# Three rearrangements of TensorE's order: branch B's values two blocks behind their transpositions, pair weights loaded one pair sooner, branch A's transpositions two tiles behind

## The chip, the cores and the metric

The kernel runs on one core of a Trainium2 chip. Its engines work side by side, each through its own list of instructions, and wait for each other by semaphores: TensorE (PE; PEld is its loading of weights) multiplies, VectorE (DVE), ScalarE (ACT) and GpSimd (POOL) do the elementwise work, and SyncE (SP) issues the transfers. SBUF is the working memory, and PSUM holds what PE writes, in banks of 512 fp32 columns. The metric is the time of one execution on the device in microseconds, as the median of several; a profile is taken of one further execution.

## What is computed

One block of an encoder: 1024 tokens of width 1024 with 16 meta tokens ahead of them, all in fp32. Two attentions stand side by side on the normed input, and what they give is mixed by gates; a feed-forward part follows.

```python
def mixer_block(h, w_in, lq1, lk1, lq2, lk2, subln_g, sink, w_ba, w_bb, w_o, lambda_init):
    proj = h @ w_in                      # qa, ka, va, qb, kb, vb, ga, gb side by side
    ...
    y_a = differential_attention(...)    # 4 heads: softmax(q1 k1) - lam * softmax(q2 k2), times v, over all keys
    y_b = windowed_gqa(...)              # 8 heads in 2 groups, each block of 128 queries sees 3 blocks of keys
    merged = jax.nn.sigmoid(ga) * (y_a @ w_ba) + jax.nn.sigmoid(gb) * (y_b @ w_bb)
    return merged @ w_o

def reference(x, meta_tokens, ...):
    ...
        h = h + mixer_block(rms_norm(h, norm_mix[layer]), ...)
        h = h + swiglu(rms_norm(h, norm_ffn[layer]), w_ff_gate[layer], w_ff_up[layer], w_ff_down[layer])
    return rms_norm(h, norm_final)[:, N_META:]
```

## The kernel before

Every fp32 operand of a matmul is split into a rounded part (hi) and a rest (lo), and a product is made of three matmuls: hi hi, hi lo, lo hi. A split costs ACT a copy (the hi) and DVE or POOL a subtraction (the lo).

The mixer runs in stages, along PE's order. First come the normed input's transposes and the projections of branch B. Then **branch B** (65 to 246 us of the profile): for each of 2 groups and 8 blocks of 128 queries, `attend_b` gives two generators. `scoring` makes four scores (L329), whose exponentials ACT takes (L337) and POOL scales (L343). `values()` transposes the result key block by key block (L363, two to three blocks and one of meta tokens) into one of two PSUM banks (tile `bpt`), copies it to SBUF as hi (ACT, L365) and lo (DVE, L367) in one of four tiles `btr`, and multiplies it by v (`products`, L357); the sum of a block lies in the bank `bpy`. While block n is scored, block n-1 is transposed and multiplied: the list `finish` holds its generator. A string of letters sets PE's order within a block: `SLOTS_B`, where s takes a step of the scores, t one of the values and g one step of fill. Fill (`more`, from `fill_b`) is work that is needed later: projections of v and k of branch A (L214) in steps of three matmuls, whose results ACT and DVE take out.

What is left of the fill follows branch B. While it runs, DVE makes `token_sums` (L608 to L621), sums of quarters of the transposed input, split into the tiles `tops`. Then come the **pair products** (`product_t`, L690; 268 to 395 us and, before them, the end of the fill): pairs of 128 columns of q of branch A and of the gates, seven products each, made by Strassen-Winograd's scheme from sums of quarters. A pair's weights are two transfers (`load_t`, L651), which DVE combines (L660 to L664) and ACT and POOL split (`wop_t`). DVE also adds up the products (L699), and so frees their banks.

**Branch A** (395 to 660 us) takes 4 heads of 8 tiles of 128 queries. A step n of the loop makes tile n's six scores (two maps of three, L785, each into one bank of a ring of five, `SC`), which DVE adds the distances to (L788), ACT takes the exponential of (L793) and, of the second map, DVE combines with the first (L799). The same step transposes an earlier tile (`transpose_a`, L811: three banks of the same ring, taken out by ACT at L814 and DVE at L815), and for every second tile `values_a` multiplies by v (L824) and `normed_a` norms (L837 to L846). The order is set by the strings `SLOTS` for the first 13 steps and `SLOTS_LAST` after them, where s is a score, t a transposition, n a step of the values or the norm, g a fill step. The first map of a tile is scored into fresh tiles, the second into one of two that alternate (`s0s`). Each head's q and k are loaded by `load_a` (L761 to L764) into single tiles that the scores of the head before must have released.

The order is written out by hand for PE alone (`manual_schedule`); that of the other engines' instructions comes from a scheduler, which may place them otherwise when PE's order changes.

Of the kernel before, what the change touches and what calls it, by code (L numbers as in the profile page):

```python
# [9 lines left out]
F32 = mybir.dt.float32  # L10
# [10 lines left out]
P = 128  # L21
# [18 lines left out]
PC_BUFS = 8  # L40
PAD_T = 192
COMBINE_POOL = (0, 1, 2, 3)
SLOTS = "sgsgsngsgsstntnt"
SLOTS_LAST = "sgssngsgsstntnt"
N_MORE = 13
SLOTS_B = "sgsgsgsggttgttgttgtt"
S_BUFS = (2, 2)
AT_BUFS = 2
G_BUFS = 3
# [8 lines left out]
QK_BUFS = 3  # L58
W_BUFS = 2
X_BUFS = 2  # L60
T_LAG = 1
V_AT = 2
B_LAST = 10
E_STEPS = 1
OP_BUFS = 8
# [13 lines left out]
def encoder_block(ctx: ExitStack, tc: tile.TileContext, x, meta, norm_mix, w_in, lq1, lk1, lq2, lk2,  # L79
# [78 lines left out]
    wpool, close_wpool = pool("wpool", "right")  # L158
# [155 lines left out]
    def attend_b(g, t, finish):  # L314
# [35 lines left out]
        def values():  # L350
# [9 lines left out]
            for k, kp, o in blocks:  # L360
                pt = bank(psum1, "bt", f"bpt_{nm}_{k}", 2).rearrange("p (r t) -> p r t", r=4)
                for r in range(4):
                    nc.tensor.transpose(pt[:kp, r, :], st[:, r, o:o + P] if k < 8 else md[:, r], ident)  # L363
                tr = bpool.tile([P, 2, 4, P], F32R, tag="btr", name=f"btr_{nm}_{k}", bufs=4)
                nc.scalar.activation(tr[:kp, 0], pt[:kp], AF.Copy)  # L365
                lo = tr[:, 1] if k < 8 else tr[:NM, 0]
                nc.vector.tensor_tensor(lo, pt[:lo.shape[0]], f32(tr[:lo.shape[0], 0]), ALU.subtract)  # L367
                trs.append((k, kp, tr))
                yield
                if len(trs) > 1:  # L370
                    products(*trs.pop(0))
                    yield
            products(*trs.pop(0))
            y1 = bpool.tile([64, 512], F32, tag="by1", name=f"by1_{nm}", bufs=2)
            nc.scalar.copy(y1, py[64:128])
# [203 lines left out]
    order_pe = tc.manual_schedule(engines={mybir.EngineType.PE})  # L579
    order_pe.__enter__()  # L580
    more = fill_b()
    for _ in finish.pop(0):
        next(more)
    for n in range(2, BG * NT):
# [60 lines left out]

    def load_t(u):
        for kh in range(2):
            p = tpool if u % 2 else wpool
            w = raw_t[u, kh] = p.tile([P, 4, 2 * P], F32, tag="w", name=f"wt_{u}_{kh}", bufs=2)
            src = w_in[kh * 512:kh * 512 + 512, units[u][0]:units[u][0] + 2 * P]  # L650
            nc.sync.dma_start(w, src.rearrange("(c p) n -> p c n", p=P))  # L651

# [46 lines left out]
            nc.vector.tensor_tensor(other, ps, other, ALU.add)  # L699
            result_t(u, *{2: (0, 0), 7: (1, 1), 3: (0, 1)}[p], other)  # L700

    load_t(0)
    load_t(1)
    for n, (u, p) in enumerate(steps_t):
        while len(ops_t) < min(len(steps_t), n + 2 * W_BUFS):
            ahead = steps_t[len(ops_t)]
            weights_t(*ahead)
            if ahead[1] == 4 and ahead[0] + 2 < len(units):
                load_t(ahead[0] + 2)
        product_t(u, p)  # L710
    order_pe.__exit__(None, None, None)
    order += order_fill
# [809 lines left out]
```

## Time and profile before

| | us |
|---|---|
| median of 3 runs (lowest to highest) | 1510.72 (1507.9 to 1513.98) |
| profiled execution | 1509.8 |
| its span, first to last instruction | 1508.0 |
| PE busy in the span | 1449.7 |
| PE busy, 65 to 246 us (branch B) | 166.7 of 181 |
| PE busy, 268 to 395 us (pair products) | 114.1 of 127 |
| PE busy, 395 to 660 us (branch A) | 255.6 of 265 |

Times within the profile are microseconds from the span's start. A row of a timeline has the start, the length, the engine, the line of the kernel, the operation, what it writes and reads, and in square brackets how long its engine was idle before it and whose result ended that. A row of the list of waits has who waits for whom, the sum in us, how often, and the longest.

### The profile page before, as it was taken

The page shows a single profiled execution, that of the slowest core. Times are in us where ns is not written, and L with a number is a line of the kernel's source. Part 1 is how long each engine was busy: PE and PEld are TensorE (multiplying, and loading weights), DVE is VectorE, ACT ScalarE, POOL GpSimd, SP SyncE. Part 2 cuts the span into 40 slices and gives each one's busy share as a digit, 9 for nine tenths or more (in the row PEclk, how much of TensorE's full clock was granted, in tenths as well). Part 3 has the DMA queues.
Part 4 walks back from the last instruction along what each step waited for, and adds up shares of the span by engine and source line. Part 5 has one row for each costly group of instructions (what it writes and reads, how often), then busy time and mean ns, then how long its engine had stood idle before and what let it go on. Part 6 is the DMA issues. An engine that isn't in the chain of part 4 may idle for free.

```text
span 1508.0 us, 21007 instructions
## 1 busy us (share of the span) xinstructions
PE 1449.7 (96%) x7315; PEld 1229.4 (82%) x7315; DVE 895.3 (59%) x1635; ACT 685.2 (45%) x1296; POOL 565.0 (37%) x555
## 2 busy tenths in 40 slices
PE   8999999799999999999999999999999999999998
PEld 7877779578898898987878878888888888888886
DVE  6456666831497787824443495655555554778666
ACT  6365654433365555625532463333333333444444
POOL 4243432544232322322663316454544453000344
PEclk9999999999999999999999999999999999999999
DMA  7424313352714424128662254333333232864443
GB/s 231 91 59 113 84 58 112 97 147 89 220 58 149 134 79 127 51 86 263 196 216 76 79 154 159 108 105 105 105 105 102 101 105 105 291 240 126 133 126 140
DMA packets 154203, 193.13 MB, mean 128 GB/s; under 512 B 16288, under 2 KB 98656, under 8 KB 154096
## 3 DMA queue, kind: packets, MB, share of 16 engines
q1 hardware_dynamic: 154096, 191.78, 40.0%
q8 instruction: 58, 0.95, 0.3%
q14 instruction: 49, 0.40, 0.1%
HBM read 131.24 MB, written 53.94 MB: 123 GB/s over the span
## 4 chain that ended last, share of the span: by engine, by line
PE 75%; DVE 7%; issue 5%; DMA 5%; POOL 4%; ACT 3%; SPq 1%; POOLq 0%; DVEq 0%; ACTq 0%
PE pg L1303 27%; PE pd L1397 8%; PE po L1069 6%; PE pp_g L214 5%; PE pt L690 5%; PE ppa L728 4%; PE aps L785 3%; PE apy L824 3%; POOL oa L121 3%; PE apt L811 2%; PE pp_qb L214 2%; PE pp_ka L214 2%; PE pp_va L214 2%; PE bpy L357 1%; DVE btr L367 1%
## 5 line engine op out<-in xcount | busy, mean ns | idle before, releaser
L1303 PE MATMUL pg<-t,wop 128*128 128x512 f32 x1056 | 243.0, 389 | 1.6 <-DVE wop L121 1.6
L1303 PEld LDWEIGHTS pg<-t,wop 128*128 128x128 f32 x1056 | 198.0, 188 | 43.3 <-DVE wop L121 2.0
L121 POOL TENSOR_TENSOR wop<-wf,wop 128x512 fp32r<-128x512 f32 x118 | 157.4, 1336 | 156.6 <-ACT wop L120 144.2
L1397 PE MATMUL pd<-ob,oa 128*128 128x512 f32 x924 | 210.2, 389 | 1.0 <-DVE ob L121 0.5
L1397 PEld LDWEIGHTS pd<-ob,oa 128*128 128x128 f32 x924 | 173.3, 188 | 37.7 <-DVE ob L121 1.0
L1303 PE MATMUL pg<-b,wop 128*128 128x512 f32 x792 | 183.2, 389 | 0.0
L1303 PEld LDWEIGHTS pg<-b,wop 128*128 128x128 f32 x792 | 148.5, 188 | 30.8
L120 ACT ACTIVATE wop<-wf 128x512 fp32r<-128x512 f32 x128 | 80.2, 632 | 82.3 <-PE pg L1303 52.0
L121 POOL TENSOR_TENSOR oa<-ra,oa 128x512 fp32r<-128x512 f32 x33 | 44.1, 1337 | 170.9 <-ACT oa L120 169.4
L793 ACT ACTIVATE as<-as,amn 128x1040 f32<-128x1040 f32 x64 | 74.5, 1164 | 54.4 <-DVE amn L788 51.0
L187 POOL TENSOR_TENSOR wl_c<-w_c,wh_c 128x512 fp32r<-128x512 f32 x48 | 61.5, 1302 | 96.0 <-ACT wh_c L184 95.7
L120 ACT ACTIVATE oa<-ra 128x512 fp32r<-128x512 f32 x77 | 48.7, 632 | 106.6 <-PE pd L1397 50.6
L1069 PE MATMUL po<-woh,mT 128*128 128x512 f32 x384 | 88.6, 391 | 0.0
L785 PE MATMUL aps<-ak,aq 128*128 128x352 f32 (+1 forms) x384 | 86.9, 329 | 1.0 <-DVE at L815 0.5
L1069 PEld LDWEIGHTS po<-woh,mT 128*128 128x128 f32 x384 | 71.7, 188 | 14.7
L1127 DVE TENSOR_TENSOR s<-wf,wf 128x512 f32<-128x512 f32 x22 | 16.4, 750 | 107.5 <-DMA wf<-in_w_ff_up_dram 52.7
L785 PEld LDWEIGHTS aps<-ak,aq 128*128 128x128 f32 x384 | 66.9, 189 | 11.2 <-issue 1.3
L121 POOL TENSOR_TENSOR wop_t<-wt,wop_t 128x512 fp32r<-128x512 f32 x30 | 49.0, 1636 | 66.5 <-ACT wop_t L120 63.5
L690 PE MATMUL pt<-tops,wop_t 128*128 128x512 f32 x240 | 58.1, 399 | 11.0 <-DVE tops L121 4.6
L343 POOL TENSOR_SCALAR bs<-bs,bdn 128x432 f32<-128x432 f32 (+1 forms) x64 | 37.1, 602 | 73.2 <-ACT btr L365 36.7
L690 PEld LDWEIGHTS pt<-tops,wop_t 128*128 128x128 f32 x240 | 45.7, 192 | 22.7 <-DVE u L699 5.1
L796 POOL TENSOR_SCALAR as<-as,adn,neglam 128x1040 f32<-128x1040 f32 x32 | 39.0, 1218 | 65.5 <-DVE adn L794 62.7
(279 smaller groups left out, 3196.0 us busy)
## 6 DMA issues: line engine op xcount, KB each, us to landing
ra<-aop SPq DMA_DIRECT2D x77, 256.0 KB, 2.6
w_c<-in_w_in_dram SPq DMA_DIRECT2D x25, 512.0 KB, 4.0
wf<-in_w_ff_gate_dram SPq DMA_DIRECT2D x24, 512.0 KB, 3.6
wf<-in_w_ff_up_dram SPq DMA_DIRECT2D x24, 512.0 KB, 3.6
aop<-as SPq DMA_DIRECT2D x44, 256.0 KB, 2.1
aop<-c SPq DMA_DIRECT2D x33, 256.0 KB, 2.0
gt<-g_d SPq DMA_DIRECT2D x32, 256.0 KB, 3.5
wt<-in_w_in_dram SPq DMA_DIRECT2D x10, 512.0 KB, 4.4
```

What stands on the lines that cost most here:

```text
L120: nc.scalar.activation(hi, src, AF.Copy)
L121: lo_eng.tensor_tensor(lo, src, f32(hi), ALU.subtract)
L187: (lo_eng or nc.gpsimd).tensor_tensor(wl[:, c], w[:, c], f32(wh[:, c]), ALU.subtract)
L214: nc.tensor.matmul(ps[:, :n], a[:, c, :], b[:, c, at:at + n], start=(c == 0 and i == 0), stop=(c == DC - 1 and i == 2))
L690: nc.tensor.matmul(ps, op[:, 4 * a + c], moving(p, c, b), start=(p in (1, 2, 5) and c == 0 and n == 0), stop=(p in (4, 2, 3) and c == 3 an ...
L728: nc.tensor.matmul(ps, w[:, a, j, :], src(j, b, tk), start=(j == 0 and n == 0), stop=(j == 3 and n == 2))
L785: nc.tensor.matmul(ps[:, :n], qs[m][:, t * P:(t + 1) * P], ks[m][:, vv, k0:k0 + n], start=(vv == 0), stop=(vv == 1))
L793: nc.scalar.activation(s[m][:, 0:L], s[m][:, 0:L], AF.Exp, bias=low, scale=-1.0, accum_out=dn[:, m:m + 1])
L824: nc.tensor.matmul(py[:, cols], v[:kp, a, k, :], at_[:kp, k, b, :], start=(k == 0 and j == 0), stop=(k == 8))
L1069: nc.tensor.matmul(ps, mT[:, c, a, t * P:(t + 1) * P], wos[q, c][:, b], start=(c == 0 and n == 0), stop=(c == DC - 1 and n == 2))
L1303: nc.tensor.matmul(ps, op[:, x, c, :], b[:, y, c, :], start=(p in (1, 2, 5) and c == 0 and n == 0), stop=(p in (4, 2, 3) and c == 3 and n ...
L1397: nc.tensor.matmul(ps[u], oa[:, a, u * P:(u + 1) * P], ob[:, b, :], start=(p in (1, 2, 5) and j == 0 and k == 0), stop=(p in (2, 3, 4) and ...
```

## The change

In branch B, `values()` makes the products of a key block once two later blocks are transposed rather than one (`len(trs) > 2`), and takes out what is left at the end. `SLOTS_B` has seven fill steps in a block rather than eight, in other places, and `B_FIRST` fill steps are taken before the first block's values, which had begun with none. In the pair products `tpool` has four buffers for weights beside the two of `wpool`, so that three pairs can be loaded at the start and pair u+3 is asked for where u+2 was. In branch A tile n-2 rather than n-1 is transposed in step n (`T_LAG`), and the strings put the transpositions between the first three scores instead of at the step's end. Work and its amount are the same. In the changed kernel the lines behind L58 have numbers higher by 1, those behind L373 by 4, those behind L583 by 6.

```diff
--- before.py
+++ after.py
@@ -40,10 +40,10 @@
 PC_BUFS = 8
 PAD_T = 192
 COMBINE_POOL = (0, 1, 2, 3)
-SLOTS = "sgsgsngsgsstntnt"
-SLOTS_LAST = "sgssngsgsstntnt"
+SLOTS = "stgstgstgsngsnsn"
+SLOTS_LAST = "stgstgstsngsnsn"
 N_MORE = 13
-SLOTS_B = "sgsgsgsggttgttgttgtt"
+SLOTS_B = "sgsgsgstgtgttgtttgt"
 S_BUFS = (2, 2)
 AT_BUFS = 2
 G_BUFS = 3
@@ -58,8 +58,9 @@
 QK_BUFS = 3
 W_BUFS = 2
 X_BUFS = 2
-T_LAG = 1
+T_LAG = 2
 V_AT = 2
+B_FIRST = 8
 B_LAST = 10
 E_STEPS = 1
 OP_BUFS = 8
@@ -367,9 +368,12 @@
                 nc.vector.tensor_tensor(lo, pt[:lo.shape[0]], f32(tr[:lo.shape[0], 0]), ALU.subtract)
                 trs.append((k, kp, tr))
                 yield
-                if len(trs) > 1:
+                if len(trs) > 2:
                     products(*trs.pop(0))
                     yield
+            while len(trs) > 1:
+                products(*trs.pop(0))
+                yield
             products(*trs.pop(0))
             y1 = bpool.tile([64, 512], F32, tag="by1", name=f"by1_{nm}", bufs=2)
             nc.scalar.copy(y1, py[64:128])
@@ -579,6 +583,8 @@
     order_pe = tc.manual_schedule(engines={mybir.EngineType.PE})
     order_pe.__enter__()
     more = fill_b()
+    for _ in range(B_FIRST):
+        next(more)
     for _ in finish.pop(0):
         next(more)
     for n in range(2, BG * NT):
@@ -645,8 +651,8 @@
 
     def load_t(u):
         for kh in range(2):
-            p = tpool if u % 2 else wpool
-            w = raw_t[u, kh] = p.tile([P, 4, 2 * P], F32, tag="w", name=f"wt_{u}_{kh}", bufs=2)
+            p, bufs = (tpool, 4) if u % 3 else (wpool, 2)
+            w = raw_t[u, kh] = p.tile([P, 4, 2 * P], F32, tag="w", name=f"wt_{u}_{kh}", bufs=bufs)
             src = w_in[kh * 512:kh * 512 + 512, units[u][0]:units[u][0] + 2 * P]
             nc.sync.dma_start(w, src.rearrange("(c p) n -> p c n", p=P))
 
@@ -699,14 +705,14 @@
             nc.vector.tensor_tensor(other, ps, other, ALU.add)
             result_t(u, *{2: (0, 0), 7: (1, 1), 3: (0, 1)}[p], other)
 
-    load_t(0)
-    load_t(1)
+    for u in range(3):
+        load_t(u)
     for n, (u, p) in enumerate(steps_t):
         while len(ops_t) < min(len(steps_t), n + 2 * W_BUFS):
             ahead = steps_t[len(ops_t)]
             weights_t(*ahead)
-            if ahead[1] == 4 and ahead[0] + 2 < len(units):
-                load_t(ahead[0] + 2)
+            if ahead[1] == 4 and ahead[0] + 3 < len(units):
+                load_t(ahead[0] + 3)
         product_t(u, p)
     order_pe.__exit__(None, None, None)
     order += order_fill
```

Three places show how the order moves; rows of fill are left out there.

PE in branch B, the values of block 3 of the first group. A name holds group, block and key block (`bpt_0_3_2` is the transposition of key block 2, 8 are the meta tokens). Before:

```order
L363 MATMUL bpt_0_3_2_1385<-ident_99,bs_0_3_1211 128x128 x4
L363 MATMUL bpt_0_3_3_1393<-ident_99,bs_0_3_1211 128x128 x4
...
L357 MATMUL bpy_0_3_1384<-btr_0_3_2_1390,vb0_130 128x512 x2
L363 MATMUL bpt_0_3_4_1406<-ident_99,bs_0_3_1211 128x128 x4
...
L357 MATMUL bpy_0_3_1384<-btr_0_3_3_1398,vb0_130 128x512 x2
L363 MATMUL bpt_0_3_8_1419<-ident_99,bmd1_133 128x128 x4
...
L357 MATMUL bpy_0_3_1384<-btr_0_3_4_1411,vb0_130 128x512 x2
L357 MATMUL bpy_0_3_1384<-btr_0_3_8_1424,vb0_130 128x512
```

And now:

```order
L364 MATMUL bpt_0_3_2_1397<-ident_99,bs_0_3_1234 128x128 x4
...
L364 MATMUL bpt_0_3_3_1415<-ident_99,bs_0_3_1234 128x128 x4
...
L364 MATMUL bpt_0_3_4_1434<-ident_99,bs_0_3_1234 128x128 x4
L358 MATMUL bpy_0_3_1396<-btr_0_3_2_1402,vb0_130 128x512 x2
...
L364 MATMUL bpt_0_3_8_1447<-ident_99,bmd1_133 128x128 x4
L358 MATMUL bpy_0_3_1396<-btr_0_3_3_1420,vb0_130 128x512 x2
L358 MATMUL bpy_0_3_1396<-btr_0_3_4_1439,vb0_130 128x512 x2
...
L358 MATMUL bpy_0_3_1396<-btr_0_3_8_1452,vb0_130 128x512
```

Each product stands one transposed block farther behind its own transposition; `btr_0_3_2` is used behind key block 4's transposition rather than behind key block 3's. In the places left out, before: one fill step ahead of each of the first three products; now: one behind each of the first two transpositions, one ahead of key block 8's and one ahead of the last product.

PE in branch A, step 22 (head 2, tile 6). A score's name holds head, tile, map and first column, a transposition's head, tile and third. Before:

```order
L785 MATMUL aps_2_6_1_0_5857<-ak2_1_5300,aq2_1_5299 128x352 x2
...
L785 MATMUL aps_2_6_1_352_5864<-ak2_1_5300,aq2_1_5299 128x352 x2
L785 MATMUL aps_2_6_1_704_5868<-ak2_1_5300,aq2_1_5299 128x336 x2
...
L785 MATMUL aps_2_6_0_0_5882<-ak2_0_5306,aq2_0_5305 128x352 x2
...
L785 MATMUL aps_2_6_0_352_5889<-ak2_0_5306,aq2_0_5305 128x352 x2
L785 MATMUL aps_2_6_0_704_5893<-ak2_0_5306,aq2_0_5305 128x336 x2
L811 MATMUL apt_2_5_0_5899<-ident_99,as0_1_3800 128x128 x4
L837 MATMUL apst_2_0_5906<-ones_104,ysq_2_0_5875 128x1 x4
L811 MATMUL apt_2_5_1_5914<-ident_99,as0_1_3800 128x128 x4
L811 MATMUL apt_2_5_2_5921<-ident_99,as0_1_3800 128x128
```

And now, up to the last score:

```order
L791 MATMUL aps_2_6_1_0_5814<-ak2_1_5265,aq2_1_5264 128x352 x2
L817 MATMUL apt_2_4_0_5818<-ident_99,as0_0_3799 128x128 x4
...
L791 MATMUL aps_2_6_1_352_5828<-ak2_1_5265,aq2_1_5264 128x352 x2
L817 MATMUL apt_2_4_1_5832<-ident_99,as0_0_3799 128x128 x4
...
L791 MATMUL aps_2_6_1_704_5842<-ak2_1_5265,aq2_1_5264 128x336 x2
L817 MATMUL apt_2_4_2_5849<-ident_99,as0_0_3799 128x128
L791 MATMUL aps_2_6_0_0_5853<-ak2_0_5271,aq2_0_5270 128x352 x2
L830 MATMUL apy_2_1_5721<-at2_2_5482,av2_5276 128x256 x9
...
L791 MATMUL aps_2_6_0_352_5869<-ak2_0_5271,aq2_0_5270 128x352 x2
L830 MATMUL apy_2_1_5721<-at2_2_5482,av2_5276 128x256 x9
L791 MATMUL aps_2_6_0_704_5882<-ak2_0_5271,aq2_0_5270 128x336 x2
```

Before, tile 5 is transposed behind tile 6's scores; now tile 4 is, between the first four scores of tile 6. Fill stands where rows are left out.

DVE in the same step. Now:

```order
L794 ISA as1_2_6_5813,amn_2_6_5811<-aps_2_6_1_0_5814,dist_811,far_a_841 128x352
...
L794 ISA as1_2_6_5813,amn_2_6_5811<-aps_2_6_1_352_5828,dist_811,amn_2_6_5811 128x352
...
L800 RECIPROCAL adn_2_5_5734<-adn_2_5_5734 128x1
L805 SCALAR_TENSOR_TENSOR as0_1_3800<-as0_1_3800,adn_2_5_5734,as1_2_5_5735 128x1040
L821 TENSOR_TENSOR at2_4_5643<-apt_2_4_0_5818,at2_4_5643 128x4x128
L821 TENSOR_TENSOR at2_4_5643<-apt_2_4_1_5832,at2_4_5643 128x4x128
L794 ISA as1_2_6_5813,amn_2_6_5811<-aps_2_6_1_704_5842,last_dist_831,amn_2_6_5811 128x336
...
L794 ISA as0_0_3799,amn_2_6_5811<-aps_2_6_0_0_5853,dist_811,far_a_841 128x352
```

The combination of tile 5 (L805) stands ahead of both rests of tile 4's transpositions (L821), and these ahead of tile 6's third score (L794).

SP, the loads of pair weights (`wt_`, pair and half). Before, from pair 2 on:

```order
L651 DMA wt_2_0_3210<-in_w_in_dram 128x4x256
L536 DMA qa_d0_63<-qk_stage_3144 64x2x512 x2
L536 DMA qa_d2_65<-qk_stage_3184 64x2x512 x2
L651 DMA wt_2_1_3212<-in_w_in_dram 128x4x256
L536 DMA qa_d1_64<-qk_stage_3249 64x2x512 x2
L651 DMA wt_3_0_3316<-in_w_in_dram 128x4x256
```

And now, from pair 0's second half on:

```order
L657 DMA wt_0_1_3090<-in_w_in_dram 128x4x256
L657 DMA wt_1_0_3092<-in_w_in_dram 128x4x256
L657 DMA wt_1_1_3094<-in_w_in_dram 128x4x256
L657 DMA wt_2_0_3096<-in_w_in_dram 128x4x256
L657 DMA wt_2_1_3098<-in_w_in_dram 128x4x256
```

Pairs 1 and 2 are now asked for in one piece right behind pair 0, and pair 2 no longer behind stores of q.

## The prediction

> **What bounds the kernel now.** I read the busy times of the whole span first, then the same by stage, then the list of TensorE's waits in each stage that the change touches, and last the timeline at the waits.
>
> ```profile
> PE 1449.7 (96%) x7315; PEld 1229.4 (82%) x7315; DVE 895.3 (59%) x1635; ACT 685.2 (45%) x1296; POOL 565.0 (37%) x555
> 65.00:246.00 181.00, 166.66 (x938) 140.32 (x937) 109.11 (x277) 107.52 (x260) 64.52 (x98) 0.99 0.31 84
> 268.00:395.00 127.00, 114.10 (x513) 94.00 (x513) 50.06 (x69) 43.84 (x75) 59.51 (x42) 0.97 0.43 126
> 395.00:660.00 265.00, 255.63 (x1618) 233.92 (x1617) 205.09 (x596) 144.05 (x270) 76.84 (x93) 0.99 0.33 103
> ```
>
> In the lines by stage the first figures are the stretch, its length and TensorE's (PE's) busy time, and the third from the end is its granted clock. PE is busy for 1449.7 of 1508.0 us. The change adds no matmul and removes none, so the time can only move by PE's idle time. In the three stretches that it edits that is 14.3 us (branch B, 65 to 246), 12.9 (the pair products, 268 to 395) and 9.4 (branch A, 395 to 660): 36.6 us in all, to be gained at most, and nothing from 870 on, where the code is the same.
>
> **Branch B.**
>
> ```profile
> PE bpy L357 <- DVE btr L367: 10.3, 29, 0.6
> 92.48 0.60 PE L363 MATMUL bpt<-ident,bmd 128*128 128x128 f32 x4
> 92.83 0.42 PE L214 MATMUL pp_va<-hT_hi,wh_c 128*128 128x384 f32 x1
> 93.17 0.60 ACT L365 ACTIVATE btr<-bpt 128x512 fp32r<-128x512 f32 x1 [0.82 <-PE bpt L363]
> 93.43 0.62 PE L357 MATMUL bpy<-btr,vb 128*128 128x512 f32 x2
> 93.80 0.68 DVE L367 TENSOR_TENSOR btr<-bpt,btr 16x512 fp32r<-16x512 f32 x1 [0.73 <-ACT btr L365]
> 94.54 0.50 PE L357 MATMUL bpy<-btr,vb 128*128 128x512 f32 x1 [0.48 <-DVE btr L367]
> 94.87 0.55 PE L329 MATMUL bps<-kb,qb 128*128 128x432 f32 x2
> ```
>
> From a transposition's start to the product that needs it there are 2.06 us: 92.48 to 94.54, through ACT's copy (0.60) and VectorE's (DVE's) rest (0.68). PE has 0.95 us of transposition and fill before the next products (92.48 to 93.43), so with one transposed block between, the product waits; 29 times, 10.3 us idle. From one product's start to the next there are 1.11 us at that place (93.43 to 94.54) for two products of some 0.25, so that a wait costs rather 0.6 than its 0.48 of idle time: 29 x 0.56 = 16, and with about 3 us behind ACT's copies some 19, an estimate; its lower end is the row's 10.3.
>
> The new order of a block is T0, fill, T1, fill, T2, P0, fill, T8, P1, P2, fill, P8 (T a transposition, P its products). A 384-wide fill step is 0.60 us (92.83 to 93.43), a transposition 0.35 (92.48 to 92.83), a pair of products some 0.5 (93.43 to 94.54 holds three and a wait; estimate from 94.54 to 94.87 for one, and 0.62 busy for two). P0 comes 3 x 0.35 + 2 x 0.60 = 2.25 us behind T0, P1 2.75 behind T1, P2 2.3 behind T2: all over 2.06, so these waits go. Two others take their place. The transpositions have two PSUM banks, so T2 waits until T0's rest has been taken out: 2 x 0.35 + 2 x 0.60 = 1.90 of 2.06, 0.16 short. And P8 follows T8 by 0.35 + 0.60 + 2 x 0.5 = 1.95, 0.1 short. Fill of 512 columns makes both nothing; fill of 272 (0.60 x 272/384 = 0.43) makes them 0.50 and 0.28. So 0 to 0.8 us per block, some 6 over 14 blocks, if ACT comes at once. It doesn't always: its exponentials, its weight splits and its copies of the fill now fall between, and I allow one such instruction (0.6 us, as the copy at 93.17) in most blocks, 8 to 10 more. 14 to 16 us against 19 are a gain of 3. Bounds: 0, if ACT's late copies make T2 and P8 wait as the products did, and 9, if ACT is in time.
>
> The eight fill steps ahead of the first finish go where PE idles at the head of the branch:
>
> ```profile
> 72.00:75.00 3.00, 2.22 (x8) 1.13 (x8) 3.00 (x14) 3.00 (x13) 0.00 (x0) 1.00 0.38 92
> 75.00:79.00 4.00, 2.45 (x9) 1.61 (x9) 1.66 (x8) 2.90 (x9) 3.26 (x7) 0.75 0.94 259
> 79.00:83.00 4.00, 4.00 (x22) 3.84 (x21) 1.50 (x3) 1.52 (x3) 4.00 (x6) 0.83 0.02 5
> 56.23 2.53 POOL L187 TENSOR_TENSOR wl_c<-w_c,wh_c 128x512 fp32r<-128x512 f32 x2 [0.83 <-ACT wh_c L184]
> ```
>
> PE idles 0.78 and 1.55 us in 72 to 79, 2.3 in all, and the clock granted behind it is 0.75 and 0.83 for 8 us, which costs about 4 x 0.25 + 4 x 0.17 = 1.7. Eight steps are 4.8 us of work, their split weights are ready at 58.8 (56.23 + 2.53), so both go: 4 us gained, at least 2.3. The steps are no new work; each block lacks one later.
>
> **The pair products.**
>
> ```profile
> PE pt L690 <- DVE tops L121: 4.6, 1, 4.6
> PE pt L690 <- DVE u L699: 3.8, 3, 1.6
> PE pt L690 <- ACT tops L120: 2.6, 1, 2.6
> PE pt L690 <- DVE qk_stage L232: 1.9, 1, 1.9
> 296.73 0.43 SPq L651 DMA_DIRECT2D wt<-in_w_in_dram  x1
> 301.77 0.69 DVE L660 TENSOR_TENSOR s<-wt,wt 128x512 f32<-128x512 f32 x1 [6.72 <-DMA wt<-in_w_in_dram]
> 303.12 2.11 PE L690 MATMUL pt<-tops,wop_t 128*128 128x512 f32 x8 [1.60 <-DVE u L699]
> ```
>
> The second half of a pair's weights is issued at 296.73 and used at 301.77; DVE stands 6.72 us at L660 for it, and L699, which frees the product's bank, is queued behind. With a third tile set, each load is issued a whole pair (7 products) earlier, and all three such waits go: -3.8. SP's cost: two more issues of 0.43 us before the pair products, behind branch B's last stores; nobody waits for those there.
>
> The waits for `tops` are DVE's chain of sums and splits, which begins when branch B ends:
>
> ```profile
> L121 DVE TENSOR_TENSOR tops<-f,tops 128x512 fp32r<-128x512 f32 x15 | 12.4, 853 | 0.0
> 289.00:293.00 4.00, 3.85 (x11) 3.10 (x12) 4.00 (x5) 0.00 (x0) 2.91 (x2) 0.62 0.36 111
> ```
>
> Of the fill, 48 steps rather than 42 are left behind branch B, so PE comes to its first `tops` six steps of 0.43 to 0.60 us, some 3 us, later after DVE began, and waits that much less. The last split of the first needed sum also stands three or four places (0.6 us each) earlier in DVE's new order: 2 more. The group's 15 splits have no idle time before them (the last figure of its row), so DVE cannot start any of them sooner in another way. Together -5 of the 4.6 + 2.6 + 1.9, between -3 and -7. The pair products thus give 9, between 6 and 12.
>
> [...]
>
> **Branch A** is where I expect to pay.
>
> ```profile
> PE apt L811 <- DVE as L799: 5.5, 5, 2.9
> PE apt L811 <- DVE adn L794: 2.9, 2, 1.6
> 551.71 0.66 PE L811 MATMUL apt<-ident,as 128*128 128x128 f32 x4 [0.74 <-DVE as L799]
> 554.81 1.30 DVE L799 SCALAR_TENSOR_TENSOR as<-as,adn,as 128x1040 f32<-128x1040 f32 x1
> 557.99 0.40 PE L214 MATMUL pp_g<-hT_hi,wh_c 128*128 128x512 f32 x1
> 558.68 0.79 PE L785 MATMUL aps<-ak,aq 128*128 128x352 f32 x4
> 559.31 0.60 PE L811 MATMUL apt<-ident,as 128*128 128x128 f32 x4
> 559.66 1.08 PE L824 MATMUL apy<-at,av 128*128 128x256 f32 x7
> 560.01 0.57 DVE L788 CUSTOM_DVE_ANT_0 as<-aps,last_dist,amn 128x336 f32<-128x336 f32 x1
> 560.50 0.16 DVE L794 RECIPROCAL adn<-adn 128x1 f32<-128x1 f32 x1
> 560.71 1.15 ACT L793 ACTIVATE as<-as,amn 128x1040 f32<-128x1040 f32 x1
> 560.85 0.69 DVE L815 TENSOR_TENSOR at<-apt,at 128x512 fp32r<-128x512 f32 x1 [0.18 <-ACT at L814]
> ```
>
> Transposing a tile two steps late removes the waits for its combination (L799) in the steady steps: 0.74 each where it stands as at 551.71, about 0.9 from start to start, three of them, and one of 1.6 to 1.7 for L794. That is -4.5. The first wait of the branch (2.9) is its start, and stays.
>
> What comes instead: the score banks are a ring of five. In a new step they are taken in the order score, T0, score, T1, score, T2, and the fourth score gets T0's bank, so it waits until T0's rest (L815) has been taken out. On DVE that rest stands behind the previous tile's combination, which waits for that tile's second exponential. From the last score's end of a step this chain is 0.57 (L788) + 1.15 (L793) + 0.16 (L794) + 1.30 (L799) + 0.69 (L815) = 3.87 us, and with some 0.3 for the readouts between them (estimate) 4.15. PE's work up to that fourth score is three scores (0.32 each, half of 558.68 to 559.31), two transpositions (0.35 each, 559.31 to 559.66), two fill steps (0.69 each, 557.99 to 558.68) and T2, a quarter of one (0.1): 3.14 us. So about 1.0 us is waited in steps before which no value product stands (1.08 us of cover, 559.66): the even tiles, seven of them from step 13 on, 7 us. For the odd ones I take 1 us together; in the first 13 steps one fill step more (0.69) lies ahead and leaves about 0.4, five times: 2. Together 10. Bounds: 3, if DVE is ahead of this chain, and 20, if the wait holds in every one of the 19 later steps with scores.
>
> ```profile
> 447.34 0.47 PE L785 MATMUL aps<-ak,aq 128*128 128x336 f32 x2
> 447.84 0.34 SPq L761 DMA_DIRECT2D aq<-qa_d  x1
> 464.12 0.40 PE L785 MATMUL aps<-ak,aq 128*128 128x352 f32 x1 [0.26 <-DMA ak<-ka_d]
> ```
>
> Between heads, q and k of the next head are loaded when the third score of the last tile has released them (447.34 + 0.32), and the next head's fourth score waits a little for the last piece at 464.12, 16.5 us later. The new order puts one fill step, two transpositions and a value product, 2.5 to 3.5 us, before that third score rather than behind it, so the cover shrinks to 13 or so: about 2.5 us more here and less at the two later boundaries, where I allow 2: +4.5 (0 to 7). Branch A: -4.5 + 10 + 4.5 = +10, between 0 and 20.
>
> **The sum.** -4 - 3 - 9 + 10 = -6 against the profiled execution, whose time is 1509.8 (its span of 1508.0 and 1.8 around it): 1503.8. The median shown, 1510.72, is 0.9 higher; I forecast 1504.
>
> **Rivals.** (1) Only the removals happen: DVE is idle often enough in branch A (205 of 265 us busy) for its chain not to decide, and the load lands in time. Then -4 - 3 - 9 - 4.5 = -20.5: 1490. For it speaks that share; against it, that DVE works in order and the 4.15 us chain stands at one place of every step. (2) Branch A's ring and loads decide: the wait of about 1 us stands in nearly all later steps, +20 and +5 for the loads less the 4.5, and branch B's gain fails but for its head: -4 + 0 - 6 + 20.5, so +10.5: 1521. It decides from the point at which more than 20 us are waited in front of fourth scores. (3) In branch B the lag is only nominal: two PSUM banks serve three transpositions, T2 waits where the product waited, and the smaller fill costs 2: then -4 + 2 - 9 + 10 = -1: 1510.
>
> **How the numbers follow.** Forecast 0.45, rival 1 0.25, rival 2 0.15, rival 3 0.15. A measurement tells changes of about 0.5% from none, 7.6 us here: faster is below 1503.2, slower above 1518.3. The forecast's own spread is 7 us to either side (1497 to 1511), nearly half of it faster: 0.20; rival 1 gives 0.25 and rival 3 0.02: 0.47. Slower: rival 2's 0.12 and 0.03 from the edges: 0.15. The rest, 0.38, is no change. The range from 1488 to 1520 takes in rivals 1 and 3 and the nearer part of rival 2.
>
> **What will show it.** Right: L358's waits for L368 under 8 us; none of DVE's at L666 for the weights over 1 us; the wait for `tops` under 3; in branch A the transposition's waits for L805 gone but for the start, and new waits of the fourth score for L821 in even tiles; a load wait of 2 to 3 us at the first boundary. Wrong: branch A's PE idle time between its start and end below 9.4 us (rival 1) or above 30 (rival 2), or more than 10 us of waits of L364 for L368 in branch B (rival 3).

## The result, and the profile after

The changed kernel took 1496.24 us in the median of 5 runs (1493.25 to 1501.51) beside 1510.72 for the kernel before; the ratio is 0.9902 with a 95% interval from 0.9875 to 0.9929. A second set of runs gave 1499.8 (1496.96 to 1502.97) and a ratio of 0.9931 (0.9914 to 0.9948). So it is about 0.7 to 1.0% faster, and both intervals are clear of no change. The forecast was 1504, no change or a little faster, in a range from 1488 to 1520.

The busy times by stage follow, before and after, with boundaries at the same places of the program and columns as in the prediction. Three of the four rows of before stand in the prediction's first fence; the fourth is the rest of the fill behind branch B:

```profile
246.00:268.00 22.00, 20.44 (x135) 20.16 (x134) 20.48 (x33) 9.00 (x18) 3.62 (x2) 1.00 0.35 113
```

And of the changed kernel:

```profile
65.00:233.25 168.25, 157.46 (x921) 136.07 (x921) 109.77 (x276) 105.92 (x258) 61.58 (x96) 1.00 0.32 85
233.25:262.30 29.05, 25.13 (x151) 24.56 (x150) 27.20 (x41) 10.19 (x20) 6.45 (x4) 0.94 0.48 148
262.30:380.60 118.30, 113.63 (x514) 94.45 (x513) 44.67 (x62) 43.77 (x75) 57.21 (x42) 0.99 0.44 125
380.60:650.25 269.65, 258.50 (x1618) 234.25 (x1617) 203.21 (x596) 148.57 (x270) 76.68 (x93) 0.99 0.33 102
```

| stage | before | after | difference | predicted |
|---|---|---|---|---|
| branch B | 181.0 | 168.25 | -12.75, of which about 3 are six fill steps that now come later | -7 |
| rest of the fill | 22.0 | 29.05 | +7.05, with those six steps | } -9 together |
| pair products | 127.0 | 118.3 | -8.7 | } |
| branch A | 265.0 | 269.65 | +4.65 | +10 |

Put together, branch B gave 9.7, the fill and the pair products 4.7 (8.7 less 7.05, and the 3 us of moved work), and branch A cost 4.7: -9.7 us up to the last value product. The spans differ by 13.5 (1508.0 and 1494.5). Most of the other 3.8 stands in the branch products (L728, now L734), whose code is the same: 92.8 us from the first to the last before (681.61 to 774.37), 89.5 after (671.87 to 761.32). An experiment below looks at that, and at how far the length of a stage in one profile can be trusted.

The waits of the changed kernel, in the three stretches (who waits for whom, us, times, longest):

```profile
PE bpt L364 <- DVE btr L368: 7.6, 8, 1.9
PE bpy L358 <- DVE btr L368: 1.5, 5, 0.6
PE pv_va L253 <- DVE va_stage L556: 3.9, 2, 3.4
PE pt L696 <- POOL wop_t L122: 1.8, 1, 1.8
PE pt L696 <- DVE tops L122: 1.8, 1, 1.8
PE pt L696 <- ACT u L700: 1.1, 1, 1.1
PE apt L817 <- DVE as L805: 4.5, 2, 2.4
PE apt L817 <- DVE adn L800: 2.9, 1, 2.9
PE aps L791 <- DMA ak<-ka_d: 2.8, 4, 0.9
PE aps L791 <- DVE at L821: 0.4, 1, 0.4
```

In branch B the product's wait went from 10.3 us to 1.5, and a wait of the transposition, for the same engine's same rest, took most of its place (7.6). Behind branch B the waits for `u` are gone but for one for ACT (1.1), the one for `qk_stage` (1.9 before) is gone, those for `tops` fell from 4.6 + 2.6 to 1.8, and two others grew there: L253's for `va_stage` (1.6 before) and one for POOL. In branch A the fourth scores wait 0.4 us for L821, where the prediction had 10. But the first two tiles wait 2.4 and 2.9 us for their combination, once more than before. The second of the two waits for L805, 2.1 us, stands at the branch's end (638.11), where before there were 1.4 and 0.4 (644.61 and 648.75). The loads cost 2.8 us in four waits, against 0.3 in one.

### The profile page after: what moved, and what is told of

It is laid out like the page before. It is cut to its first block, busy times and chain, and to the rows that moved or that the text cites. A ratio compares the mean times of both kernels' runs of the same rounds, so it can differ in the third digit from the quotient of the medians.

```text
span 1494.5 us, 21017 instructions
## 1 busy us (share of the span) xinstructions
PE 1446.2 (97%) x7315; PEld 1229.3 (82%) x7315; DVE 896.1 (60%) x1635; ACT 689.9 (46%) x1296; POOL 563.0 (38%) x555
## 4 chain that ended last, share of the span: by engine, by line
PE 74%; DVE 7%; DMA 6%; issue 5%; POOL 3%; ACT 3%; SPq 1%; POOLq 0%; DVEq 0%; ACTq 0%
PE pg L1309 27%; PE pd L1403 8%; PE po L1075 6%; PE pt L696 5%; PE pp_g L215 5%; PE ppa L734 4%; PE aps L791 3%; PE apy L830 3%; POOL oa L122 3%; PE pp_qb L215 2%; DMA ak<-ka_d 2%; PE apt L817 2%; PE bpy L358 1%; PE pp_ka L215 1%; PE pp_va L215 1%
## 5 line engine op out<-in xcount | busy, mean ns | idle before, releaser
L799 ACT ACTIVATE as<-as,amn 128x1040 f32<-128x1040 f32 x64 | 74.5, 1164 | 64.9 <-DVE amn L794 50.8
L791 PE MATMUL aps<-ak,aq 128*128 128x352 f32 (+1 forms) x384 | 92.4, 332 | 3.4 <-DMA ak<-ka_d 2.8
L215 PE MATMUL pp_g<-hT_hi,wh_c 128*128 128x512 f32 x160 | 68.9, 431 | 0.0
L215 PE MATMUL pp_g<-hT_hi,wl_c 128*128 128x512 f32 x160 | 63.3, 395 | 0.0
```

The costliest lines, as they stand in the source:

```text
L215: nc.tensor.matmul(ps[:, :n], a[:, c, :], b[:, c, at:at + n], start=(c == 0 and i == 0), stop=(c == DC - 1 and i == 2))
L791: nc.tensor.matmul(ps[:, :n], qs[m][:, t * P:(t + 1) * P], ks[m][:, vv, k0:k0 + n], start=(vv == 0), stop=(vv == 1))
L799: nc.scalar.activation(s[m][:, 0:L], s[m][:, 0:L], AF.Exp, bias=low, scale=-1.0, accum_out=dn[:, m:m + 1])
```

## The experiments

Each ran beside the kernel before on the same chip, and ratios are to that kernel.

**The three parts, one at a time, and two together.** `b_alone` is the kernel before with `values()`, `SLOTS_B` and `B_FIRST` of the change; `pairs_alone` with `load_t` and its calls; `a_alone` with these:

```diff
-SLOTS = "sgsgsngsgsstntnt"
-SLOTS_LAST = "sgssngsgsstntnt"
+SLOTS = "stgstgstgsngsnsn"
+SLOTS_LAST = "stgstgstsngsnsn"
-T_LAG = 1
+T_LAG = 2
```

`without_a` is the changed kernel with that piece taken back.

> Branch B's part alone (values two blocks behind, seven fill steps, eight ahead of the first finish); weights and branch A as before. If the parts add up as the stages of the two profiles read, branch B ends 12 to 13 us earlier, 3 of which are six fill steps that come later, and the whole gains 8 to 10 us: 1501 to 1503. Rival: the pair products wait for the sums of quarters all the longer, because PE is there sooner, and give half of it back: a gain of 4 to 5, 1506. The prediction had 7 for this part.

> The earlier pair loads alone. Theory: the three waits for L699 behind L660's wait for the weights go, 3.8 us and little else: 1506 to 1507. Rival: DVE's waits for the weights also hold up the sums of quarters, and the gain is 7 or more. Second rival: the loads, put ahead of other transfers, delay what is stored and loaded there, and nothing is gained.

> Branch A's transpositions two tiles behind, alone. The prediction's step gives +10 us (1521). What the profile of the changed kernel shows for branch A is +4.7 us from the first score to the last value product (1515 or 1516 in all). Rival: branch A's own loss is an accident of what precedes it, and alone it gains the 4.5 us of removed waits: 1506.

> The change with branch A's part undone (branch B and the pair loads stay). If branch A costs 4.7 us in it, this is 1491 to 1492, faster than both kernels. If branch A's part pays (for instance by what comes behind it, where 3.3 us are gained up to the last branch product), it is 1496 or slower.

| kernel | median, us | ratio to before (95%) |
|---|---|---|
| before | 1510.04 | |
| b_alone | 1501.45 | 0.9934 (0.9916 to 0.9952) |
| pairs_alone | 1505.11 | 0.9962 (0.9949 to 0.9976) |
| a_alone | 1514.9 | 1.003 (1.0018 to 1.0043) |
| without_a | 1494.95 | 0.9891 (0.9875 to 0.9907) |

Branch B's part gains 8.6 us, the pair loads 4.9, and branch A's part costs 4.9. The first two sum to 13.5, and together they give 15.1. In `pairs_alone` the three waits for L699 are gone and nothing else is; those for `tops` are unchanged, and so is the one for `qk_stage` (1.8):

```profile
PE pt L690 <- DVE tops L121: 4.6, 1, 4.6
PE pt L690 <- ACT tops L120: 2.7, 1, 2.7
```

In `a_alone`, branch A and its neighbourhood (396 to 667 us) have the waits of the changed kernel, though the rest is that of before. Two of them:

```profile
PE apt L811 <- DVE adn L794: 2.9, 1, 2.9
PE aps L785 <- DMA ak<-ka_d: 2.5, 3, 1.1
```

So the 2.9 us wait at the second tile belongs to branch A's part, and so do the three load waits, which all stand at the two later boundaries between heads.

**Does branch A's part cost as much inside the change?** The changed kernel and the one without branch A's part, once more and on one chip.

> The changed kernel once more, beside the next one on the same chip. If branch A's part costs about 5 us in it, as it does alone, it is 5 us above the kernel without that part; if the parts help each other, less than 2.

> Branch B's part and the pair loads once more: 5 us below the changed kernel by the first theory, within 2 by the second.

They took 1499.8 (0.9931, 0.9914 to 0.9948) and 1495.54 us (0.9902, 0.9885 to 0.992): 4.3 us apart, as alone. In the first sets, which did not run beside each other, it was 1.3. The intervals overlap, so this pair alone does not settle the amount. The profiles do: from the first score of branch A to the last value product, the four with branch A's part (two of the changed kernel, `a_alone` and `head13` below) take 264.5 to 266.8 us, and the ten without it, of before and of all other experiments, 258.6 to 263.2. The means are 5.0 apart. With `a_alone`, whose interval is clear of no change, the cost is 4 to 5 us.

**What the second block of distance does by itself.** `lag_alone` is the kernel before with

```diff
-                if len(trs) > 1:
+                if len(trs) > 2:
                     products(*trs.pop(0))
                     yield
+            while len(trs) > 1:
+                products(*trs.pop(0))
+                yield
             products(*trs.pop(0))
```

> The kernel before with nothing but the second transposed block between transposition and product in branch B (no other string, no fill ahead of the first finish). If the distance in blocks is what counts, the 10.3 us of L357's waits for L367 go and 5 us or more are gained: 1505 or less. If two banks decide, T2 now comes 1.3 us behind T0 (two transpositions and a fill step), 0.7 short of the 2.06 that T0's rest takes, and the last product 0.6 short: 1.3 us in each of 14 blocks, as before, and 0 to 2 us are gained; the waits stand at L363 for L367.

It took 1507.82 us, a ratio of 0.9985 (0.9976 to 0.9994). Its waits in branch B:

```profile
PE bpt L363 <- DVE btr L367: 13.2, 16, 1.9
PE bpy L357 <- DVE btr L367: 0.3, 2, 0.2
```

The product's 10.3 us of waiting fell to 0.3, and the transposition's rose from nothing to 13.2: the wait moved to the two banks. Its cost did not stay the same, though. The first score of the third block and that of the last, in the kernel before and then in `lag_alone`:

```profile
84.49 0.55 PE L329 MATMUL bps<-kb,qb 128*128 128x432 f32 x2
224.51 0.29 PE L329 MATMUL bps<-kb,qb 128*128 128x288 f32 x1
86.11 0.36 PE L329 MATMUL bps<-kb,qb 128*128 128x432 f32 x1
222.64 0.42 PE L329 MATMUL bps<-kb,qb 128*128 128x288 f32 x2
```

Between the two there are 140.0 us before (and in the three other profiles with branch B as before) and 136.5 with the distance alone, for the same matmuls. So these 13 blocks gain 3.5 us. The head of the branch, from its first score to the third block's, took 20.7 us rather than 17.8 to 19.0, with a new wait of 1.9 us for L367. How much of the 8.6 us the moved fill gives by itself was not measured; the distance alone gave the whole kernel 1.6.

**A third bank.** `three_banks` is `without_a` with

```diff
-    N_PP = [3]
+    N_PP = [2]
-                pt = bank(psum1, "bt", f"bpt_{nm}_{k}", 2).rearrange("p (r t) -> p r t", r=4)
+                pt = bank(psum1, "bt", f"bpt_{nm}_{k}", 3).rearrange("p (r t) -> p r t", r=4)
```

and the same count of three at the other place that uses these banks (the input's transposes).

> Branch B's part and the pair loads, with three PSUM banks for the transpositions in branch B rather than two, and two rather than three for the fill and the projections before it. Theory: the waits of L364 for L368 (7.2 us idle, 9.0 from start to start) come from the two banks, and go: branch B ends 7 to 9 us earlier after its first score, if the fill can do with two banks. Rival: the transposition's wait moves to the products (L358) or the fill waits for a bank instead: no gain or a loss, in the projections ahead of branch B too.

It took 1491.28 us (1489.8 to 1495.06), a ratio of 0.9873 (0.9853 to 0.9893): the lowest median here, 4.3 us under `without_a_again` of the same chip, with intervals that overlap a little. The longest wait left in its branch B, and the first scores of the third and of the last block:

```profile
PE bpy L358 <- DVE btr L368: 2.7, 5, 1.2
85.31 0.36 PE L330 MATMUL bps<-kb,qb 128*128 128x432 f32 x1
206.90 0.29 PE L330 MATMUL bps<-kb,qb 128*128 128x288 f32 x1
```

The transposition's wait for L368 is gone, and the 13 blocks take 121.6 us rather than the 127.1 of the changed kernel (below). So two banks were what was left of the wait in branch B. From the first score to the last product there are 161.0 us (64.41 to 225.40), against 165.3 in the changed kernel (66.65 to 231.91) and 166.4 in `without_a`: 4 to 5 us less, where 7 to 9 were expected. A part comes back behind it, where the fill now has two banks:

```profile
PE pp_ka L215 <- DVE va_stage L556: 8.0, 2, 5.1
PE pt L696 <- DVE qk_stage L233: 1.7, 1, 1.7
```

**Work for the wait behind branch B.** `three_first` is `without_a` with

```diff
-    steps_t = [(u, p) for u in range(2) for p in (1, 2)]
-    steps_t += [(u, p) for u in range(2) for p in (6, 5, 7, 3, 4)]
-    steps_t += [(u, p) for u in range(2, len(units)) for p in (1, 2, 6, 5, 7, 3, 4)]
+    steps_t = [(u, p) for u in range(3) for p in (1, 2)]
+    steps_t += [(u, p) for u in range(3) for p in (6, 5, 7, 3, 4)]
+    steps_t += [(u, p) for u in range(3, len(units)) for p in (1, 2, 6, 5, 7, 3, 4)]
```

and `banks_six` is `three_banks` with one step less of fill in a block:

```diff
-SLOTS_B = "sgsgsgstgtgttgtttgt"
+SLOTS_B = "sgsgsstgtgttgtttgt"
```

In `banks_six` the last columns of q of branch B's second group are projected and loaded (up to 193 us) behind the first scores that read them (180.7 us), so it computes a part of the block wrongly; the amount of work is the same.

> Branch B's part and the pair loads, and products 1 and 2 of a third pair (which need no sums of quarters; its weights are loaded ahead now) put before the first product that needs them: 24 matmuls, 5.5 us of work. Theory: DVE's chain of sums sets when that product can start, about 44 us behind branch B, so the work goes into PE's waits there (1.9 and 2.1 us, and the clock behind them) and 4 to 5 us are gained against the kernel without branch A's part. Rival: the wait is POOL's split weights, which come later by as much: no gain.

> The kernel with three banks, and one fill step fewer in each block (six, the third one between the scores left out), so that 14 more steps, some 7.7 us of work, stand behind branch B, where DVE's chain of sums sets the pace. Theory: PE waits 10 us there (at L253, L215 and L696) and takes the steps for nothing, while branch B has slack with three banks: 4 us faster than with three banks alone, about 1487. Rival: the waits come back in branch B as large as the step that is missing, 0.5 us per block: no gain.

`three_first` took 1494.61 us (0.989, 0.9871 to 0.9909), 0.9 from `without_a_again`: not to be told from no gain. The wait for `tops` is gone, and POOL's wait, 1.8 us in `without_a`, grew in its place, as the rival had it:

```profile
PE pt L696 <- POOL wop_t L122: 3.9, 1, 3.9
```

`banks_six` took 1499.39 us (0.9925, 0.9912 to 0.9939), 8 us more than `three_banks`, though on another chip. Its waits behind branch B are no smaller for the 14 more steps (the first row is a new wait within branch B):

```profile
PE bps L330 <- DMA qb<-qk_stage: 3.7, 2, 2.9
PE pp_va L215 <- DVE va_stage L556: 5.0, 1, 5.0
PE pp_ka L215 <- DVE va_stage L556: 3.6, 1, 3.6
PE pv_va L253 <- DVE qk_stage L233: 1.3, 1, 1.3
```

Behind branch B they are 9.9 us, as with three banks alone (8.0, 1.7 and one of 0.2). From the last product of branch B to the first score of branch A there are 159.3 us (229.65 to 388.98), against 152.0 (225.40 to 377.40): 7.3 more for the 14 steps, some 7.7 us of work. My theory, that fill is free there, falls, at least with two banks for it. The waits name what holds it: each fill step ends in a rest that DVE takes out (L556, L233), and this rest stands in the same queue as the sums. In branch B the late load of q, the first row, hides what the missing step would give.

**The loads between heads.** `head13` is the changed kernel with

```diff
-G_HEAD = 10
+G_HEAD = 13
```

> The changed kernel with 13 fill steps rather than 10 ahead of each later head (the same fill in all, three steps per head taken from the end). 2.1 us more cover at each boundary, against waits for the loads of 0.5, 1.1 and 1.2 us from start to start: 2 to 3 us less, if the loads are what branch A's part costs at the boundaries. Rival: the fill is missing in the last steps, where DVE is behind, and as much is waited there.

It took 1498.03 us (0.9915, 0.9901 to 0.9929), between the two medians of the changed kernel. Its waits in branch A:

```profile
PE apt L817 <- DVE adn L800: 2.9, 1, 2.9
PE apt L817 <- DVE as L805: 2.7, 2, 2.4
PE aps L791 <- DVE at L821: 1.0, 2, 0.8
```

The waits for the loads, 2.8 us in the changed kernel, are gone: at the later boundaries between heads the shrunken cover is what caused them. In the later steps, where the fill is now missing, the waits for L821 rose by some 1 us, as the rival has it, but the 2.1 us for L805 at the end fell to 0.3. All waits of the branch together fell from 11.0 to 7.7 us. The stage fell by less, from 265.5 and 266.0 us in the two profiles of the changed kernel to 264.5: behind the wait of 0.8 us at 634.42 the granted clock fell here, to 0.72 in 634 to 640 us (the row below); in the first profile of the changed kernel it is 1.00 there.

```profile
634.00:640.00 6.00, 5.04 (x25) 4.11 (x26) 5.09 (x14) 2.56 (x6) 2.27 (x4) 0.72 0.09 34
```

0.28 of 6 us are 1.7, an estimate. So the 2 to 3 us that were expected came as waits, and half of them went again with the clock. The median of the whole does not tell, since this execution was also 2.7 us later at its last branch-B product (234.56 us, against 231.91), where the code is the same.

**The wait in the branch products.** `before_again` is the kernel before with a comment added.

> The kernel before, profiled once more. In the branch products (L728) its first profile has one wait of 2.5 us for split weights (wbha) that is 0.5 to 1.3 in every other kernel, whose code is the same there. If the wait belongs to the kernel it stands again with 2 us or more; if it is one execution's transfer, it is about 1.

```profile
PE ppa L728 <- POOL wbha L121: 1.4, 1, 1.4
```

It is 1.4 us, where the first profile of the same kernel has:

```profile
PE ppa L728 <- POOL wbha L121: 2.5, 1, 2.5
```

So the length of this wait changes from execution to execution, and the first profile caught a long one. The branch products took 90.2 us here (684.38 to 774.61), 2.5 less than in the first profile of the same kernel. The wait is 1.1 of that. The rest is the clock: around the longer wait (759.82) it fell in the first profile. Over the branch products 0.98 was granted there, and 1.00 in the second profile and in the changed kernel's.

```profile
756.00:764.00 8.00, 5.53 (x18) 4.10 (x18) 4.23 (x6) 3.72 (x6) 8.00 (x6) 0.79 0.51 173
```

0.21 of 8 us are 1.7, an estimate. So of the 13.5 us between the two profiled spans, 2.5 are one execution's own and no part of the change. The other way round, branch A took 262.8 us here, 2.0 more than in the first profile: a stage's length from one profile is good to 2 or 3 us.

## Why the prediction was right, and where not

The range held the time, and the sign of each of the three parts was right. The likeliest time was 8 us too high, and branch A's term was the one most wrong. That the sum of -6 came within 4 us of the -9.7 of the stages is in part luck: the pair products gave 4 us less than forecast, branch A cost 5 less, and these two errors cancel.

Of the signs of being right, L358's waits for L368 (1.5), the wait for `tops` (1.8) and the end of L805's waits in the steady steps came, and none of the signs of being wrong did. Three others did not come. DVE still waits 2.1 us for weights at L666 (293.71), though PE waits for nothing behind it; the fourth score waits 0.4 us for L821; and the first boundary in branch A waits 0.3 us for its load, the two later ones 0.9 each.

**Branch B, -4 - 3.** Alone it gave 8.6, so the sum is near, but not its two terms. The same two scores as above, in the changed kernel:

```profile
85.72 0.36 PE L330 MATMUL bps<-kb,qb 128*128 128x432 f32 x1
212.82 0.42 PE L330 MATMUL bps<-kb,qb 128*128 128x288 f32 x2
```

The 13 blocks take 127.1 us rather than 140.0, with 43 matmuls fewer, which at 0.13 to 0.17 us from start to start are some 6.5. So the blocks gained about 6.4, where the term had 3. The head, from the first score to the third block's, has the eight steps, 24 matmuls or 4.1 us, more and takes 18.6 to 21.9 us in the profiles with this part against 17.8 to 19.0 in those without: a gain of 2 to 3, where the term had 4.

The working holds in one point: the product's distance to its transposition now covers the 2.06 us, and the 10.3 us went to 1.5. The second, that two banks make T2 wait, I priced at 0.16 us per block plus what ACT adds, with P8's wait 14 to 16 us in all; the two waits are 9.1 us, of which the transposition has 7.6 in 8 places, up to 1.9. The rows of the first block show why one is long (a timeline of the changed kernel):

```profile
78.56 1.07 ACT L185 ACTIVATE wh_c<-w_c 128x1024 fp32r<-128x1024 f32 x1 [3.42 <-DMA w_c<-in_w_in_dram]
80.53 0.58 ACT L366 ACTIVATE btr<-bpt 128x512 fp32r<-128x512 f32 x1
81.15 0.69 DVE L368 TENSOR_TENSOR btr<-bpt,btr 128x512 fp32r<-128x512 f32 x1 [1.92 <-ACT btr L366]
81.99 0.63 PE L364 MATMUL bpt<-ident,bmd 128*128 128x128 f32 x4 [1.77 <-DVE btr L368]
```

ACT stands 3.42 us for the next weights of the fill (L185), then takes out a fill result (79.53) and an exponential (79.89), and begins the copy of key block 0, transposed at 78.14, at 80.53 only; key block 8's transposition needs that bank. I had looked whether the eight moved steps have their own weights in time, and not that the steps behind them ask for theirs earlier too, in a queue that the transposition's copy shares. This wait of 1.77 us is about as much as the head gave less than forecast. That two banks make T2 wait the prediction named as its third rival; it is a part of the case, not all of it, and `three_banks` shows what it was worth: 5.5 us in the 13 blocks.

**The bound of 36.6 us of idle time** was no bound. In branch B the idle time fell from 14.3 to 10.8 us, 3.5, while the stage lost 9.7 beside the moved work. PE's busy time fell as well, by 9.2 from 166.66 to 157.46, for 17 matmuls fewer, which at some 0.17 us are 3. Another 1.7 (an estimate, 0.09 of 19) are the clock at the head, 0.91 in 65 to 84 us before and 1.00 after. For a part of the rest, a product behind a wait counts as busy for longer than in a stream: 0.50 us in the prediction's row at 94.54, and here, without a wait,

```profile
231.91 0.40 PE L358 MATMUL bpy<-btr,vb 128*128 128x512 f32 x1
```

So idle time understates here what a wait costs. The step that counted 0.56 us from start to start for each of the 29 waits, rather than the row's 0.35, was in the right direction.

**The pair products, -9**, gave 4.7. The pair loads were right: 3.8 predicted, 4.9 measured alone, and in the change one wait for `u`, of 1.1 us, is left of the 3.8. What failed is the other term, "-5 of the 4.6 + 2.6 + 1.9". PE does come to its first `tops` later, and these three waits fell by 7.3, from 9.1 to 1.8, more than forecast. But the step took for granted that no other wait grows, and two did: L253's for `va_stage` from 1.6 to 3.9, ahead of the sums, and one of 1.8 for POOL's split weights right behind them (277.93). Together the five fell from 10.7 to 7.5, by 3.2. Around L253's wait the row of 253 to 259 us (shown at the end) has DVE busy for 6.00 of 6.00: the fill's own rests stand in the queue in which the sums are made, as `banks_six` has it too. What is left, about 1 us, went with PE's busy time, and no run gives a cause.

The granted clock is low behind the waits of this stage in both kernels, and the forecast's sum has no term for it. Before, 0.62 was granted from 284 to 293 us, of which PE was busy for 4.35; now it is 0.72 from 253 to 259 (PE busy for 5.20) and 0.66 from 278 to 283 (5.00). By these numbers an estimated 1.7 us were lost before (0.38 of 4.35) and 3.2 now (0.28 of 5.20 and 0.34 of 5.00). The 1.5 more may be what is left above; no run shows it.

**Branch A, +10**, cost 4.3 to 4.9. Three steps of it can be told apart.

That "the fourth score gets T0's bank" is wrong. In the even tile 2 of head 2 the changed kernel shows

```profile
502.52 0.08 DVE L794 DVE_READ_ACCUMULATOR2_ANT amn<- 128x1 f32 x1
502.52 0.69 DVE L821 TENSOR_TENSOR at<-apt,at 128x512 fp32r<-128x512 f32 x1
502.66 0.59 PE L791 MATMUL aps<-ak,aq 128*128 128x352 f32 x2
```

The fourth score starts at 502.66, when the readout of the second score has just ended, and T0's rest, which began at 502.52, still runs. So it did not get T0's bank. Of the five banks, T0's, T1's and the third score's were not taken out yet, and T2, which began at 502.42, had the first score's; only the second score's is left. The program's allocation does not go round the five banks in turn, and I had not looked which bank it gives. That step was worth 10 us; L821's waits are 0.4.

The removed waits, -4.5: the three of the steady steps and the one of 1.6 are gone indeed, 3.8 us of waits, but the list has 7.4 us for L805 and L800 together, 8.4 before for L799 and L794. A second wait at the start came in their place, and the waits at the end, 1.8 before, are one of 2.1:

```profile
408.91 1.09 PE L817 MATMUL apt<-ident,as 128*128 128x128 f32 x4 [2.85 <-DVE adn L800]
408.00:412.50 4.50, 3.59 (x14) 3.26 (x15) 3.39 (x8) 1.44 (x3) 1.40 (x2) 0.62 0.59 160
638.11 1.20 PE L817 MATMUL apt<-ident,as 128*128 128x128 f32 x9 [2.10 <-DVE as L805]
```

With one more step between a tile's scores and its values, PE has little but scores and fill for one step longer, and DVE falls behind it twice: at the first tile (2.4 us) and here (2.85). From 394 to 408.5 DVE is busy for 13.15 of 14.5 us, the third of the busy times in this row:

```profile
394.00:408.50 14.50, 11.28 (x67) 10.39 (x67) 13.15 (x41) 10.11 (x18) 5.34 (x6) 0.88 0.18 49
```

The clock granted behind this wait is 0.62 for 4.5 us, which costs some 1.7 more (an estimate, 0.38 of 4.5); behind the first wait it falls too (0.63 from 394 to 398), as it did before (0.57 from 408 to 412). "The first wait of the branch (2.9) is its start, and stays" was the place to ask whether a longer start has a second one.

The +4.5 for the loads was 1.8, 0.9 at each of the two later boundaries. The two profiles of the changed kernel and `a_alone` have 1.5 to 2.5 us of waits there, the ten profiles without this part none, and `head13` shows that the shrunken cover is the cause. The first boundary, which was to be the largest, waits 0.3 us as before. The fourth wait, 0.7 us at the start of the branch (386.59), does not come from this part: `without_a` has 0.9 there and `b_alone` 1.7.

Added up, 2.85 and 1.7 at the second tile, 1.8 and 0.7 for the loads, 0.3 at the end, less 3.8 in the steady steps and 0.5 at the first tile, these are some 3 of the 4.7 us. For the rest no run gives a cause.

**The rest.** Of the difference between the profiled spans 3.8 us lie behind branch A: 850.2 us from its last value product to the end before, 846.4 after. In the second profiles of the two kernels it is 847.9 and 847.2. So most of the 3.8 is one execution's own. The medians of the parts sum to -8.6, the change has -14.5 in one set of runs and -10.6 in the other; what part of this is the parts helping each other and what is the scatter of the medians stays open.

## What to carry to other kernels

A longer distance between producer and consumer paid here only as far as the buffers between them went: 1.6 us alone, with 13.2 us of waits for two banks, and 5.5 us more in 13 blocks with a third bank. Count the banks or tiles that the new distance holds open, and who empties them. Before a wait is put on a ring's next user, look up which buffer the program in fact gives it, and whom the present waits name. Ask of work that is put into a wait whether the engine that is waited for has a part in it: DVE takes out the fill behind branch B, and 14 more steps of it there took 7.3 us. The deeper pipeline of branch A had a longer start, with waits of 2.4 and 2.9 us at its first two tiles where before there was one of 2.9. A shorter wait need not shorten the whole, as in `three_first`, where POOL's wait grew from 1.8 to 3.9 us as the one for `tops` went: look which wait comes next behind it, and take a second profile before a difference of 2 or 3 us in one stage is put down to a change.

## What the runs showed that I had not expected

Waits shorter than the one of 4.6 us for `tops` before (0.62 granted from 284 to 293) have a lower clock behind them too. Around and behind the wait of 2.85 us at 408.91, 0.62 was granted for 4.5 us. The first row below is the wait of 2.38 us at the first tile (394.71), with 0.63; the second is two of 1.77 and 1.83 us shortly behind each other (275.60 and 277.93), with 0.66; the last is the wait of 3.40 us at L253 (253.80), with 0.72.

```profile
394.00:398.00 4.00, 3.29 (x16) 3.22 (x17) 2.75 (x10) 2.04 (x4) 1.39 (x2) 0.63 0.41 117
278.00:283.00 5.00, 5.00 (x15) 3.98 (x16) 5.00 (x4) 1.53 (x4) 4.95 (x3) 0.66 0.00 0
253.00:259.00 6.00, 5.20 (x24) 5.20 (x25) 6.00 (x12) 1.87 (x4) 0.00 (x0) 0.72 0.32 107
```

A wait of some 2 us does not have it each time: around the one of 2.10 us at 638.11 the clock granted from 625 to 650 us is 1.00.
